# Gated DeltaNet in a hybrid decoder trunk: channel-major outputs by swapped operands, norm factors applied late through DRAM

## The chip, the cores and the metric

The kernel runs on one core of a Trainium2 chip. The metric is the device time of one execution in microseconds; lower is better. A core has five engines with instruction queues of their own, each working in order: TensorE (PE, matrix products; its weight loads are listed as PEld), VectorE (DVE), ScalarE (ACT), GpSimd (POOL) and SyncE (SP, which here only issues DMA transfers; ACT and POOL issue some too).

## The reference, cut to what matters

One layer: RMS norm of 528 tokens (16 learned meta tokens and 512) of width 2048, one input projection, three groups of heads (gated DeltaNet 6 × 128, GLA 5 heads, forgetting attention "FoX" 5 heads), each with a SiLU gate, and one output projection with the residual and a last norm. All is fp32. The change lies in DeltaNet, whose output is normed and gated per head:

```
def gated_head_norm(o, z, w):
    o = o * lax.rsqrt(jnp.mean(o * o, axis=-1, keepdims=True) + EPS) * w
    return o.reshape(z.shape) * jax.nn.silu(z)
...
        v_new = u_c - jnp.einsum('bhck,bhkv->bhcv', w_c, s)
        o = jnp.einsum('bhck,bhkv->bhcv', qd, s) + jnp.einsum('bhcs,bhsv->bhcv', qk_c, v_new)
        s = s * gl[..., None, None] + jnp.einsum('bhck,bhcv->bhkv', kd, v_new)
```

The norm is a factor for each token and head; w is a factor for each channel; silu(z) has one value per channel and token.

## The kernel before, in words

The input projection runs in blocks of 128 columns, `pp20`, `pp21` and so on, each in two halves of the contraction. A half's weights come as 512 KB (`raw`, issued by SP at L144), ACT rounds them to a high part (`whi`, L167), DVE makes the rest (`wlo = raw − whi`, L168), and PE does 48 products of 264 columns (or 24 of 512) with them at L242: high by high, high by the input's rest, low by high. `raw`, `whi` and `wlo` have two buffers each, so the next half's weights can be loaded and split while one is in use, and not before. PE takes projection products nearly all the time; the small products of the mixers are put between them. That order, and the one on every engine, is set when the program is built, by a scheduler's simulated times with a few tables of places (`PLACE`, `waits`, `sooner`); on the chip each engine follows its list and waits for semaphores. A dependency of the kind NoSync, in the code, only sets the order in a list and makes nothing wait.

DeltaNet runs in two groups of three heads, g = 0 and 1: `dn_keys`, `dn_values`, `dn_queries`, `dn_inverse`, `dn_mix`. While one group is mixed, the projections of the next are already under way. In `dn_keys` DVE makes the columns of decays (`cols`, L704 to L709) and with them the chunks' lower triangles `an` (L723). `dn_inverse` writes `an` to DRAM (`scr`, ACT's DMAs at L735) and reads it back as rows of small triangles (`ab`, L740); POOL fills ab's diagonal with ones (L744), and DVE inverts the triangles by steps (L749, L753). POOL's and DVE's other work stands around that: `stc5` on POOL, the convolution products `cv5` (L612, L614) and the next weight halves on DVE.

`dn_mix` goes over four blocks of 128 tokens: `pks` (keys by state), the correction `zz` on DVE, `py`, the state's update, and the output products `po`, of two products per head, token-major: tokens on partitions and channels along the row. ACT squares po with an accumulator (L975) and the norm's factors come from short DVE and ACT instructions; ACT scales po by them (L984). One block later, `gated` transposes each head on PE (`pt`, L902) and multiplies it by the channel weight and by the gate `zsdz`, which is channel-major, on DVE (L905). When a group is done, SP stores its three gates' rows to DRAM (`zd`, L1362), from where the output projection reads them.

The query's squared sums use a tile `qs` (one buffer, about the width of three heads) and a 128x128 matrix `fold`, which adds every fourth group of partitions; `fold` is made from the identity at L832 and L833 and lies in the tile `vpm`. Its product is `pq` (L891).

GLA works on pairs of heads. In `gla_pair` DVE makes the scaled keys and queries `kq` for spans of 64, 32, 16 and so on tokens (L1060 to L1067), and PE multiplies them to `pss` in four runs, `pss00` to `pss03` for the first pair (of two heads each, as `pss000` and `pss001`). POOL multiplies at L1111 and L1129 there.

Of the kernel before, what the change touches and what calls it, by code (L numbers as in the profile page):

```python
# [83 lines left out]
def tile_hybrid_trunk(ctx, tc, xT, x_first, w_first, xtok, mtok, w_gate, w_in, w_out, w_dn, consts, lmask, fin_w, out, dbg=None):  # L84
# [642 lines left out]

    def dn_inverse(g, st):
# [15 lines left out]
        G.memset(ab[:, 0:1024:33], 1.0)  # L744
        a3 = ab.rearrange("p (a c) -> p a c", a=32)
        for j in range(1, 31):
            m = 31 - j
            t3 = ot[:, : m * j].rearrange("p (a c) -> p a c", a=m)
            x = V.tensor_tensor(out=t3, in0=a3[:, j + 1 :, j : j + 1].to_broadcast([NN * 4 + H, m, j]),  # L749
                                in1=a3[:, j : j + 1, 0:j].to_broadcast([NN * 4 + H, m, j]), op=ALU.mult)  # L750
# [110 lines left out]
    def dn_mix(g, st):  # L861
# [37 lines left out]
        def gated(b):  # L899
            pt = psm.tile([P, 512], F32, tag="m", name=f"pt{g}{b}")  # L900
            for j in range(H):
                PE.transpose(pt[:, j * P : (j + 1) * P], ons[b][:, j, :], ident)  # L902
            for j in range(H):
                o = zs["dz", H * g + j][:, b * P : (b + 1) * P]
                V.scalar_tensor_tensor(out=o, in0=pt[:, j * P : (j + 1) * P], scalar=dnws[:, 0:1], in1=o,  # L905
                                       op0=ALU.mult, op1=ALU.mult)
# [9 lines left out]
        def scores(b):  # L916
            ts = bsl(b)
            p1 = psm.tile([P, 512], F32, tag="m", name=f"pa{g}{b}")
            for j in range(H):
# [2 lines left out]
            V.tensor_tensor(out=atb, in0=p1[:, : H * P].rearrange("p (h d) -> p h d", h=H), in1=atb, op=ALU.mult)
# [8 lines left out]
        scores(0)
        for b in range(NB):
            ts, eg, egl = bsl(b), egs[b], egls[b]
# [32 lines left out]
            if b:  # L966
                gated(b - 1)
            po = psm.tile([P, 512], F32, tag="m", name=f"po{g}{b}")
            for j in range(H):
# [1 line left out]
                PE.matmul(pj, at[:, b * H + j, :], y[:, j, :], start=True, stop=False)
# [8 lines left out]
            V.tensor_tensor(out=f1, in0=f1, in1=f2, op=ALU.add)  # L980
            A.activation(f1, f1, AF.Exp, scale=-0.5)
            on = t15(f"on{g}{b}")
            for j in range(H):
                A.activation(on[:, j, :], po[:, j * P : (j + 1) * P], AF.Copy, scale=f1[:, j : j + 1])  # L984
# [363 lines left out]
    for g in range(2):  # L1348
# [12 lines left out]
        for h in range(H * g, H * g + H):  # L1361
            nc.sync.dma_start(out=zd[h], in_=zs["dz", h])  # L1362
# [368 lines left out]
```

## Time and profile before

| what | us |
|---|---|
| three runs, median (lowest to highest) | 966.07 (965.44 to 967.99) |
| the profiled execution | 966.72 |
| its span, first to last instruction | 964.8 |
| PE busy | 955.4 |
| DVE busy | 688.2 |
| ACT busy | 474.5 |
| POOL busy | 233.0 |

The TensorE clock was granted in full (0.999). The span is what the trace covers; 1.9 us of the execution lie outside it. PE's busy time overlaps itself from one product to the next, since they are pipelined; what a product costs is the distance to the start of the next one.

### The profile page before, as it was taken

The numbers are of one execution on the slowest core, as the hardware profiler recorded it, in microseconds if no ns is written. First come the engines' busy times: TensorE is split into PE (matmuls) and PEld (weight loads), VectorE is DVE, ScalarE is ACT, GpSimd is POOL, SyncE is SP. The second block draws the span as 40 slices with busy tenths as digits, with TensorE's granted clock in tenths as the row PEclk, the third lists the DMA queues.
The fourth block names the chain that finished last, engine by engine and source line by source line (L and its number), as shares of the span: only waits on it lengthen the run. The fifth ranks groups of instructions, "written<-read, shape, count | busy, mean of one in ns | idle before, by whom it ended". The sixth has DMA issues, their size and how long they took to land.

```text
span 964.8 us, 18868 instructions
## 1 busy us (share of the span) xinstructions
PE 955.4 (99%) x7271; PEld 882.4 (91%) x7271; DVE 688.2 (71%) x1491; ACT 474.5 (49%) x1004; POOL 233.0 (24%) x262
## 2 busy tenths in 40 slices
PE   9999999999999999999999999999999999999996
PEld 8899999899999988899999989899999998888885
DVE  5467777878658886634685857968867758986664
ACT  7754433344446333433545554655655645544345
POOL 0033322233124235211112223232433120000023
PEclk9999999999999999999999999999999999999999
DMA  9835577978558787743747675678776588366535
GB/s 355 298 136 209 180 205 212 287 227 227 171 167 221 226 233 192 188 119 83 186 133 179 158 185 180 187 216 225 190 210 175 181 285 281 131 218 217 178 128 175
DMA packets 70334, 191.86 MB, mean 199 GB/s; under 512 B 14077, under 2 KB 17325, under 8 KB 69476
## 3 DMA queue, kind: packets, MB, share of 16 engines
q1 hardware_dynamic: 46048, 152.64, 45.5%
q0 software_dynamic: 15104, 31.66, 18.5%
q10 hardware_dynamic: 9092, 6.36, 2.5%
q8 instruction: 57, 0.93, 0.4%
q14 instruction: 33, 0.27, 0.1%
HBM read 179.94 MB, written 60.88 MB: 250 GB/s over the span
## 4 chain that ended last, share of the span: by engine, by line
PE 97%; DVE 1%; DMA 1%; ACT 0%; issue 0%; POOL 0%; ACTq 0%; SPq 0%; DVEq 0%; POOLq 0%
PE pp L242 48%; PE pp_a L569 8%; PE pq L1452 6%; PE pp L321 5%; PE pa L1452 3%; PE pt L1452 3%; PE ps L1452 3%; PE pp_b L569 2%; PE pp_c L569 2%; PE pp_d L569 2%; PE pr L1452 1%; PE pss L1087 1%; PE pfo L1328 1%; PE pfa L1279 1%; PE pgate L415 1%; PE pg L716 1%
## 5 line engine op out<-in xcount | busy, mean ns | idle before, releaser
L242 PE MATMUL pp<-xh,whi 128*128 128x264 f32 (+2 forms) x1120 | 269.6, 305 | 0.0
L242 PE MATMUL pp<-xl,whi 128*128 128x264 f32 (+2 forms) x1120 | 269.6, 305 | 0.0
L242 PE MATMUL pp<-xh,wlo 128*128 128x264 f32 (+2 forms) x1120 | 268.4, 305 | 0.2 <-DVE wlo L168 0.2
L167 ACT CAST whi<-raw 128x1024 fp32r<-128x1024 f32 x131 | 137.2, 1047 | 158.8 <-PE pp L242 97.3
L168 DVE TENSOR_TENSOR wlo<-raw,whi 128x1024 fp32r<-128x1024 f32 x131 | 165.0, 1260 | 62.6 <-ACT whi L167 59.9
L242 PEld LDWEIGHTS pp<-xh,whi 128*128 128x128 f32 x1120 | 181.2, 188 | 8.9 <-issue 0.3
L242 PEld LDWEIGHTS pp<-xl,whi 128*128 128x128 f32 x1120 | 181.5, 189 | 8.4
L242 PEld LDWEIGHTS pp<-xh,wlo 128*128 128x128 f32 x1120 | 181.1, 189 | 8.8 <-DVE wlo L168 0.5
L374 POOL TENSOR_SCALAR stc<-cv 128x528 f32<-128x528 f32 (+1 forms) x18 | 29.0, 1614 | 104.1 <-DVE cv L614 88.1
L614 DVE SCALAR_TENSOR_TENSOR cv<-pb,cpk,cv 128x528 f32<-128x528 f32 (+1 forms) x54 | 40.8, 756 | 0.6
L168 DVE TENSOR_TENSOR wlos<-raws,whis 128x1024 fp32r<-128x1024 f32 x20 | 24.2, 1222 | 14.6 <-ACT whis L167 14.6
L167 ACT CAST whis<-raws 128x1024 fp32r<-128x1024 f32 x20 | 20.7, 1049 | 26.8 <-PE pq L1452 12.5
L321 PE MATMUL pp<-xh,wf 128*128 128x512 f32 x128 | 33.1, 398 | 0.0
L1481 POOL TENSOR_TENSOR acc<-acc,fw 128x512 f32<-128x512 f32 x4 | 6.1, 1544 | 107.9 <-DVE wll L168 107.9
L569 PE MATMUL pp_a<-t,whi 128*128 128x264 f32 (+1 forms) x224 | 29.7, 282 | 0.0
L321 PEld LDWEIGHTS pp<-xh,wf 128*128 128x128 f32 x128 | 24.2, 190 | 5.6
L569 PE MATMUL pp_a<-xl,whi 128*128 128x264 f32 x112 | 28.5, 287 | 0.0
L569 PE MATMUL pp_a<-xh,whi 128*128 128x264 f32 x112 | 28.4, 286 | 0.0
L569 PEld LDWEIGHTS pp_a<-t,whi 128*128 128x128 f32 x224 | 27.8, 188 | 0.1
L363 DVE TENSOR_TENSOR pb<-pp,rstd 128x264 f32<-128x264 f32 (+1 forms) x36 | 13.8, 424 | 18.1 <-PE pp L242 18.0
L374 POOL TENSOR_SCALAR stdz<-zdz 128x512 f32<-128x512 f32 x6 | 11.2, 1874 | 62.5 <-DMA ti<-in_w_in 50.0
L481 POOL DMA_DIRECT2D tw<-tw x16 | 13.4, 835 | 51.7 <-DVE wlo L168 25.3
(497 smaller groups left out, 2072.8 us busy)
## 6 DMA issues: line engine op xcount, KB each, us to landing
raw<-in_w_in SPq DMA_DIRECT2D x103, 512.0 KB, 3.9
ti<-in_w_in SPq DMA_DIRECT2D x28, 512.0 KB, 5.2
raw<-ti SPq DMA_DIRECT2D x28, 512.0 KB, 3.5
tw<-in_w_dn SPq DMA_DIRECT2D x20, 512.0 KB, 5.3
raws<-tw SPq DMA_DIRECT2D x15, 512.0 KB, 4.0
ti<-in_w_in POOLq DMA_DIRECT2D x14, 512.0 KB, 6.3
ti<-ti POOLq DMA_DIRECT2D x14, 512.0 KB, 6.3
tw<-in_w_dn POOLq DMA_DIRECT2D x10, 512.0 KB, 6.6
```

The source lines that it names most:

```text
L167: pace[0] = A.copy(hi, raw).ins
L168: pace[1] = V.tensor_tensor(out=lo, in0=raw, in1=hi.bitcast(F32), op=ALU.subtract).ins
L242: mm = PE.matmul(p_[:, :nt], wt[:, j * m : (j + 1) * m], xx[k][:, t0 : t0 + nt], start=(k == 0 and wt is hi and xx is xh), stop=(k == KT - ...
L321: PE.matmul(begun[i][0][0][:, :S], wt[:, i * P : (i + 1) * P], xx[k][:, NM:T], start=k + n == 0, stop=k == KT - 1 and n == 2)
L363: V.tensor_tensor(out=o, in0=p_[rows], in1=rstd[rows, t0 : t0 + n], op=ALU.mult)
L374: maxes.append(G.tensor_scalar_max(t, src, LOW).ins)
L415: PE.matmul(pgate[a][:, :HT], wg[k // 8][:, k % 8, :], xx[k][:, a * HT : (a + 1) * HT], start=(k == 0 and xx is xh), stop=(k == KT - 1 and ...
L481: x = G.dma_start(out=out_[s], in_=in_[s], accum_op=ALU.add, max_dma_last_dim=2048)
L569: m = PE.matmul(p_[:, cols], wt[:, j * P : (j + 1) * P], xx[j][part_][:, cols], start=first and i == 0, stop=i == len(todo) - 1, skip_grou ...
L614: V.scalar_tensor_tensor(out=c, in0=pb[:, t0 + w : w + T], scalar=cwc[:, blk, w : w + 1], in1=c, op0=ALU.mult, op1=ALU.add)
L716: PE.matmul(pg[:r, j * r : (j + 1) * r], kT[:, j, ts], kT[:, j, ts], start=True, stop=True)
L1452: mm = PE.matmul(p_, o_[:, s], w_, start=(first and n == 0), stop=(last and n == 2), skip_group_check=True)
```

## The change

In `dn_mix` the two operands of the output products change places: `y` and the state are the stationary operands, and `at` and `eg` the moving ones, so po comes out channel-major. The gate is then multiplied into it at once, without the norm: `zb` gets po × channel weight × gate, in one DVE instruction per block. For the norm, DVE transposes po in blocks of 32x32 into `ot`, ACT squares it, and DVE sums 32 at a time (`squares`); the sums of all four blocks are folded by one product `pqo` per group (`normed`), which replaces the chain per block. The 12x128 factors are transposed (`pf`), copied (`ft`), stored to DRAM by four SP transfers (`fd`) and read back spread over all partitions (`fb`, 128x1536) into the buffer of tag "qs". POOL multiplies the gates by them in `gate` (three products of 128x512), and SP stores the result. For the first group that is done at once; for the second it is written behind the scores of GLA's first pair, with a NoSync dependency on the last `kq`.

Three smaller moves go with it: `fold` is made inside the tile `qs` instead of `vpm`; ab's diagonal is filled by DVE; the copy of the decays `egl` and POOL's product with `eg` come behind the corrections `zz`, and `squares` of a block behind those of the next.

```diff
+    factors = []
+
+    def gate(behind):
+
+        for g, zt, fb in factors:
+            for j in range(H):
+                x = G.tensor_tensor(out=zt[:, j, :S], in0=zt[:, j, :S], in1=fb[:, j], op=ALU.mult)
+                if behind:
+                    tc.add_manual_dep(x.ins, behind.name, mybir.DependencyInfo(
+                        mybir.DependencyClass.NoSync, mybir.DependencyReason.DATA), reason="behind")
+            for j in range(H):
+                nc.sync.dma_start(out=zd[H * g + j], in_=zt[:, j, :S])
+        factors.clear()
+
@@ -741,7 +755,7 @@
-        G.memset(ab[:, 0:1024:33], 1.0)
+        V.memset(ab[:, 0:1024:33], 1.0)
@@ -824,14 +838,10 @@
-        vpm3 = t15(f"vpm{g}")
+        vpm3 = t15(f"vpm{g}", (P, 2, P))
         vpm = vpm3[:, 0]
         vms = vpm3[:, 1]
         G.memset(vms, 0.0)
-        fold = vpm3[:, 2].rearrange("p (i a) -> p i a", i=4)
-        V.reduce_sum(fold[:, 0], ident.rearrange("p (i a) -> p a i", a=32), axis=mybir.AxisListType.X)
-        V.tensor_copy(fold[:, 1:], fold[:, 0].unsqueeze(1).to_broadcast([P, 3, 32]))
-        st["fold"] = vpm3[:, 2]
@@ -874,12 +884,28 @@
+        def squares(b):
+
+            return V.reduce_sum(st["sums"][:, 4 * H * b : 4 * H * (b + 1)],
+                                ots[b].rearrange("p h (i c) -> p (h i) c", c=32), axis=mybir.AxisListType.X)
+
+        zt = triples["dz", g]
-            sums = qs[:, H * S : H * S + 16 * H].rearrange("p (h m) -> p h m", h=H)
+            sums, st["sums"], st["fold"] = (qs[:, H * S + a : H * S + b] for a, b in ((0, 16 * H), (16 * H, 32 * H), (32 * H, 32 * H + P)))
+            f4 = st["fold"].rearrange("p (i a) -> p i a", i=4)
+            V.reduce_sum(f4[:, 0], ident.rearrange("p (i a) -> p a i", a=32), axis=mybir.AxisListType.X)
+            V.tensor_copy(f4[:, 1:], f4[:, 0].unsqueeze(1).to_broadcast([P, 3, 32]))
@@ -896,14 +922,31 @@
-        def gated(b):
-            pt = psm.tile([P, 512], F32, tag="m", name=f"pt{g}{b}")
-            for j in range(H):
-                PE.transpose(pt[:, j * P : (j + 1) * P], ons[b][:, j, :], ident)
-            for j in range(H):
-                o = zs["dz", H * g + j][:, b * P : (b + 1) * P]
-                V.scalar_tensor_tensor(out=o, in0=pt[:, j * P : (j + 1) * P], scalar=dnws[:, 0:1], in1=o,
-                                       op0=ALU.mult, op1=ALU.mult)
+        def normed():
+
+            pq = psm.tile([P, 512], F32, tag="m", name=f"pqo{g}")
+            PE.matmul(pq[:, : 16 * H], st["fold"], st["sums"], start=True, stop=True)
+            for i in range(4):
+                r = slice(32 * i, 32 * i + 32)
+                A.copy(so_[r], pq[r, : 16 * H].rearrange("p (b h i) -> p b h i", h=H, i=4)[:, :, :, i])
+            f1, f2 = f_[:, 0], f_[:, 1]
+            V.tensor_tensor(out=f2, in0=f2, in1=so_, op=ALU.mult)
+            A.activation(f2, f2, AF.Ln, scale=1.0 / (P * P), bias=eps_c)
+            V.tensor_tensor(out=f1, in0=f1, in1=f2, op=ALU.add)
+            A.activation(f1, f1, AF.Exp, scale=-0.5)
+            pf = psm.tile([P, 512], F32, tag="m", name=f"pf{g}")
+            PE.transpose(pf[: NB * H, :P], f1.rearrange("p b h -> p (b h)"), ident)
+            ft = t15(f"ft{g}", (NB * H, P))
+            A.copy(ft, pf[: NB * H, :P])
+            fd = drp.tile([H, NB, P], F32, name=f"fd{g}")
+            for b in range(NB):
+                nc.sync.dma_start(out=fd[:, b], in_=ft[b * H : b * H + H])
+            fb = wk.tile([P, 2 * T + 2 * S], F32, tag="qs", bufs=1, name=f"fb{g}")[:, : H * S]
+            fb = fb.rearrange("p (h t) -> p h t", h=H)
+            nc.sync.dma_start(out=fb, in_=fd.rearrange("h b t -> h (b t)").partition_broadcast(P))
+            factors.append((g, zt, fb))
+            if g == 0:
+                gate(None)
@@ -923,14 +966,11 @@
-            egl = wk.tile([P, H], F32, tag="egl", name=f"egl{g}{b}")
-            V.tensor_copy(egl, eg[:, :, P - 1])
-            G.tensor_tensor(out=eg, in0=eg, in1=qT[:, :, ts], op=ALU.mult)
-            egs[b], egls[b] = eg, egl
@@ -938,8 +978,13 @@
+                x = V.scalar_tensor_tensor(out=z[:, j, :], in0=pk[:, j * P : (j + 1) * P], scalar=nbg[:, b, j : j + 1],
+                                           in1=vp[:, b * H + j, :], op0=ALU.mult, op1=ALU.add)
+            egl = wk.tile([P, H], F32, tag="egl", name=f"egl{g}{b}")
+            behind(V.tensor_copy(egl, eg[:, :, P - 1]), x)
+            G.tensor_tensor(out=eg, in0=eg, in1=qT[:, :, ts], op=ALU.mult)
+            if b:
+                behind(squares(b - 1), x)
@@ -963,29 +1008,22 @@
-            if b:
-                gated(b - 1)
             po = psm.tile([P, 512], F32, tag="m", name=f"po{g}{b}")
             for j in range(H):
                 pj = po[:, j * P : (j + 1) * P]
-                PE.matmul(pj, at[:, b * H + j, :], y[:, j, :], start=True, stop=False)
-                PE.matmul(pj, eg[:, j, :], sst[:, j, :], start=False, stop=True)
-            for j in range(H):
-                sq = wk.tile([P, P], BF16, tag="sq", name=f"sqo{g}{b}{j}")
-                A.activation(sq, po[:, j * P : (j + 1) * P], AF.Square, accum_out=so_[:, b, j : j + 1])
-
-            f1, f2 = f_[:, 0, b, :], f_[:, 1, b, :]
-            V.tensor_tensor(out=f2, in0=f2, in1=so_[:, b, :], op=ALU.mult)
-            A.activation(f2, f2, AF.Ln, scale=1.0 / (P * P), bias=eps_c)
-            V.tensor_tensor(out=f1, in0=f1, in1=f2, op=ALU.add)
-            A.activation(f1, f1, AF.Exp, scale=-0.5)
-            on = t15(f"on{g}{b}")
-            for j in range(H):
-                A.activation(on[:, j, :], po[:, j * P : (j + 1) * P], AF.Copy, scale=f1[:, j : j + 1])
-            ons[b] = on
+                PE.matmul(pj, y[:, j, :], at[:, b * H + j, :], start=True, stop=False)
+                PE.matmul(pj, sst[:, j, :], eg[:, j, :], start=False, stop=True)
+            ot = t15(f"ot{g}{b}")
+            V.transpose(ot.rearrange("p h t -> p (h t)"), po[:, : H * P])
+            zb = zt[:, :, b * P : (b + 1) * P]
+            V.scalar_tensor_tensor(out=zb, in0=po[:, : H * P].rearrange("p (h t) -> p h t", h=H), scalar=dnws[:, 0:1],
+                                   in1=zb, op0=ALU.mult, op1=ALU.mult)
+            A.activation(ot, ot, AF.Square)
+            ots[b] = ot
             if b < NB - 1:
                 sst = sn
-        gated(NB - 1)
+        squares(NB - 1)
+        normed()
@@ -1100,6 +1138,8 @@
+        if p == 0:
+            gate(kqs[-1])
@@ -1358,8 +1398,6 @@
-        for h in range(H * g, H * g + H):
-            nc.sync.dma_start(out=zd[h], in_=zs["dz", h])
```

What the orders become, at three places. First PE, at the second block of the first group, where `pt00` are the transposes of block 0's output (columns: line, operation, out<-in, shape, times). Before:

```order
L242 MATMUL pp20_0_3504<-xl4_222,whi20_0_3509 128x264
L957 MATMUL psn01_2342<-y01_2340,kd0_1056 128x128 x3
L920 MATMUL pa02_2350<-qT0_1663,kT0_672 128x128 x3
L902 MATMUL pt00_2361<-ident_79,on00_2324 128x128 x3
L971 MATMUL po01_2368<-y01_2340,at0_1057 128x128
L972 MATMUL po01_2368<-sn00_2292,eg01_2301 128x128
L971 MATMUL po01_2368<-y01_2340,at0_1057 128x128
L972 MATMUL po01_2368<-sn00_2292,eg01_2301 128x128
L971 MATMUL po01_2368<-y01_2340,at0_1057 128x128
L972 MATMUL po01_2368<-sn00_2292,eg01_2301 128x128
L242 MATMUL pp20_1_3505<-xl4_222,whi20_0_3509 128x264
```

After:

```order
L242 MATMUL pp20_0_3462<-xl4_222,whi20_0_3467 128x264
L1002 MATMUL psn01_2333<-y01_2331,kd0_1056 128x128 x3
L963 MATMUL pa02_2341<-qT0_1661,kT0_672 128x128 x3
L1014 MATMUL po01_2349<-at0_1057,y01_2331 128x128
L1015 MATMUL po01_2349<-eg01_2301,sn00_2292 128x128
L1014 MATMUL po01_2349<-at0_1057,y01_2331 128x128
L1015 MATMUL po01_2349<-eg01_2301,sn00_2292 128x128
L1014 MATMUL po01_2349<-at0_1057,y01_2331 128x128
L1015 MATMUL po01_2349<-eg01_2301,sn00_2292 128x128
L242 MATMUL pp20_1_3463<-xl4_222,whi20_0_3467 128x264
```

The three transposes are gone, and the six output products have the same places with their operands exchanged.

Then DVE in the second group, around the columns of decays and the diagonal of `ab1`; `wlo25_0` is the low part of the first half of block 25. Before:

```order
L706 COPY cols1_3042<-cols1_3042 128x12
L706 COPY cols1_3042<-cols1_3042 16x3
L707 COPY cols1_3042<-cols1_3042 128x12
L707 COPY cols1_3042<-cols1_3042 16x3
L839 COPY cols1_3042<-cols1_3042 16x1 x2
...
L612 TENSOR_SCALAR cv5_4015<-pb5_3898,cpk_90 128x512
L614 SCALAR_TENSOR_TENSOR cv5_4015<-pb5_3898,cpk_90,cv5_4015 128x512 x3
L168 TENSOR_TENSOR wlo25_0_4561<-raw25_0_4557,whi25_0_4560 128x1024
L749 TENSOR_TENSOR ab1_4026<-ab1_4026 51x30
L753 TENSOR_TENSOR ab1_4026<-ab1_4026 51x30
```

After:

```order
L706 COPY cols1_3002<-cols1_3002 128x12
L706 COPY cols1_3002<-cols1_3002 16x3
L906 TENSOR_REDUCE qs1_4209<-ident_79 128x32
L707 COPY cols1_3002<-cols1_3002 128x12
L707 COPY cols1_3002<-cols1_3002 16x3
...
L612 TENSOR_SCALAR cv5_3973<-pb5_3856,cpk_90 128x512
L758 MEMSET ab1_3984 51x32
L614 SCALAR_TENSOR_TENSOR cv5_3973<-pb5_3856,cpk_90,cv5_3973 128x512 x3
L168 TENSOR_TENSOR wlo25_0_4475<-raw25_0_4471,whi25_0_4474 128x1024
L763 TENSOR_TENSOR ab1_3984<-ab1_3984 51x30
L767 TENSOR_TENSOR ab1_3984<-ab1_3984 51x30
```

The fold's reduction now stands inside the chain of `cols`, where it needs the buffer in which `fb0` lay; the fill stands ahead of three products of `cv5` and of `wlo25_0`, where before DVE's first touch of `ab1` came behind them.

Last POOL, from the masks `at1` of the second group on; `zsdz0` are the first group's gates. Before:

```order
L695 AFFINE_SELECT at1_3035<-at1_3035 128x384 x2
L486 DMA ti_669<-ti_669 256x512
L695 AFFINE_SELECT at1_3035<-at1_3035 128x384
L374 TENSOR_SCALAR stc4_3892<-cv4_3887 128x512
L830 MEMSET vpm1_3215 128x128
L849 COPY vpm1_3215<-v3_3223 128x16
L849 COPY vpm1_3215<-v4_3362 128x16
L849 COPY vpm1_3215<-v5_3501 128x16
L732 MEMSET ab1_4026 51x1024
L486 DMA ti_669<-ti_669 256x512
L744 MEMSET ab1_4026 51x32
L374 TENSOR_SCALAR stc5_4020<-cv5_4015 128x512
```

After:

```order
L695 AFFINE_SELECT at1_2995<-at1_2995 128x384 x2
L734 TENSOR_TENSOR zsdz0_527<-zsdz0_527,fb0_2454 128x512 x3
L695 AFFINE_SELECT at1_2995<-at1_2995 128x384
L374 TENSOR_SCALAR stc4_3850<-cv4_3845 128x512
L844 MEMSET vpm1_3175 128x128
L859 COPY vpm1_3175<-v3_3181 128x16
L859 COPY vpm1_3175<-v4_3320 128x16
L859 COPY vpm1_3175<-v5_3459 128x16
L746 MEMSET ab1_3984 51x1024
L486 DMA ti_669<-ti_669 256x512
L374 TENSOR_SCALAR stc5_3978<-cv5_3973 128x512
```

The three products with `fb0` come ahead of the last mask, of `stc4` and of all that follows; the fill has left the queue, so that `stc5` no longer stands behind it.

More of the change, by code (lines that the diff above doesn't have):

```diff
@@ L752, in dn_inverse @@
                 waits.append((x.ins, len(splits) + 2, splits))
-            V.tensor_tensor(out=a3[:, j + 1 :, 0:j], in0=a3[:, j + 1 :, 0:j], in1=t3, op=ALU.add)
+            x = V.tensor_tensor(out=a3[:, j + 1 :, 0:j], in0=a3[:, j + 1 :, 0:j], in1=t3, op=ALU.add)
         sc2 = drp.tile([NN * 4, 1024], F32, tag="sc2", name=f"sc2{g}", bufs=2)
@@ L876, in dn_mix, with behind @@
         f_ = wk.tile([P, 2, NB, H], F32, tag="ff", name=f"ff{g}")
-        egs, egls, ons = {}, {}, {}
+        egs, ots = {}, {}
+        def behind(x, y):
+            tc.add_manual_dep(x.ins, y.ins.name, mybir.DependencyInfo(
+                mybir.DependencyClass.NoSync, mybir.DependencyReason.DATA), reason="behind")
+        def squares(b):
+            return V.reduce_sum(st["sums"][:, 4 * H * b : 4 * H * (b + 1)],
+                                ots[b].rearrange("p h (i c) -> p (h i) c", c=32), axis=mybir.AxisListType.X)
+        zt = triples["dz", g]
         def query_sums():
             qs = wk.tile([P, 2 * T + 2 * S], F32, tag="qs", bufs=1, name=f"qs{g}")
-            sums = qs[:, H * S : H * S + 16 * H].rearrange("p (h m) -> p h m", h=H)
+            sums, st["sums"], st["fold"] = (qs[:, H * S + a : H * S + b] for a, b in ((0, 16 * H), (16 * H, 32 * H), (32 * H, 32 * H + P)))
+            f4 = st["fold"].rearrange("p (i a) -> p i a", i=4)
+            V.reduce_sum(f4[:, 0], ident.rearrange("p (i a) -> p a i", a=32), axis=mybir.AxisListType.X)
+            V.tensor_copy(f4[:, 1:], f4[:, 0].unsqueeze(1).to_broadcast([P, 3, 32]))
+            sums = sums.rearrange("p (h m) -> p h m", h=H)
             for j in range(H):
@@ L925, in scores @@
             A.activation(eg, eg, AF.Exp)
-            egl = wk.tile([P, H], F32, tag="egl", name=f"egl{g}{b}")
-            V.tensor_copy(egl, eg[:, :, P - 1])
-            G.tensor_tensor(out=eg, in0=eg, in1=qT[:, :, ts], op=ALU.mult)
-            egs[b], egls[b] = eg, egl
+            egs[b] = eg
         scores(0)
         for b in range(NB):
-            ts, eg, egl = bsl(b), egs[b], egls[b]
+            ts, eg = bsl(b), egs[b]
             pk = psm.tile([P, 512], F32, tag="m", name=f"pks{g}{b}")
@@ L940, in dn_mix @@
             for j in range(H):
-                V.scalar_tensor_tensor(out=z[:, j, :], in0=pk[:, j * P : (j + 1) * P], scalar=nbg[:, b, j : j + 1],
-                                       in1=vp[:, b * H + j, :], op0=ALU.mult, op1=ALU.add)
+                x = V.scalar_tensor_tensor(out=z[:, j, :], in0=pk[:, j * P : (j + 1) * P], scalar=nbg[:, b, j : j + 1],
[5 more added lines that the diff above has]
+                behind(squares(b - 1), x)
             py = psm.tile([P, 512], F32, tag="m", name=f"py{g}{b}")
```

## The prediction

> **What bounds the kernel now.** I read the page's head first, then the chain that ended last, then what TensorE (PE) waits for.
>
> ```profile
> span 964.8 us, 18868 instructions
> PE 955.4 (99%) x7271; PEld 882.4 (91%) x7271; DVE 688.2 (71%) x1491; ACT 474.5 (49%) x1004; POOL 233.0 (24%) x262
> ...
> PE 97%; DVE 1%; DMA 1%; ACT 0%; issue 0%; POOL 0%; ACTq 0%; SPq 0%; DVEq 0%; POOLq 0%
> ```
> ```profile
> PE warm L310 <- POOL ones L115: 1.2, 1, 1.2
> PE pp L242 <- DVE wlo L168: 0.2, 1, 0.2
> PE pp_b L569 <- ACT whi L167: 0.2, 1, 0.2
> ```
>
> PE is busy 955.4 of 964.8 us, 97% of the chain is PE, and after the start it waits 0.4 us in all. So the time is the sum of PE's steps. A saving on DVE, ACT or POOL is worth nothing; PE work taken away is worth its step; and any new wait of PE is paid in full, since PE has no idle time that could take it up.
>
> **The PE work.** Behind block 1's state update the rows read (a busy figure overlaps the next row, so the step is the difference of starts):
>
> ```profile
> 266.79 0.49 PE L902 MATMUL pt<-ident,on 128*128 128x128 f32 x3
> 267.12 0.39 PE L971 MATMUL po<-y,at 128*128 128x128 f32 x2
> ```
> ```profile
> L902 PE MATMUL pt<-ident,on x24: 270/273/273, 266.8 to 476.5; 128*128 128x128 f32 x24
> ```
> ```profile
> L891 PE MATMUL pq<-qs,vpm x4: 208/242/276, 247.4 to 425.7; 128*128 128x48 f32 x4
> ```
>
> Three transposes take 267.12 − 266.79 = 0.33 us, 0.11 each; 24 go: −2.66 us. Swapping the operands of the output products leaves their count and shapes (128x128 both ways). Added per group are one 128x48 product with the fold matrix (the L891 kind, two passes of at most 0.14 by its two rows per group and 276 ns) and one transpose (0.11): +0.72 in all, a little under the most that these rows allow. PE's sum falls by 1.94 us; half of it, 0.97, lies in each group. At no cover at all that is the most the change can give, but for the 0.4 us of waits above.
>
> **Work beside PE, per block.** It removes three gatings, three squares with their accumulator reads and three scaled copies; it adds a 32x32-block transpose of 128x384, one gating of 128x384, one 128x384 square and one reduction.
>
> ```profile
> L905 DVE SCALAR_TENSOR_TENSOR zsdz<-pt,dnws,zsdz x24: 329/343/351, 267.6 to 477.3; 128x128 f32<-128x128 f32 x24
> L984 ACT ACTIVATE on<-po,ff x24: 346/367/373, 259.4 to 473.6; 128x128 f32<-128x128 f32 x24
> ```
> ```profile
> L767 DVE STREAM_TRANSPOSE iv<-iv x2: 578/580/581, 213.7 to 383.6; 128x384 f32<-128x384 f32 x2
> ```
> ```profile
> L922 DVE TENSOR_TENSOR at<-pa,at x8: 549/550/557, 241.6 to 454.6; 128x384 f32<-128x384 f32 x8
> L889 DVE TENSOR_REDUCE qs<-qs x6: 670/672/675, 218.3 to 392.1; 128x16 f32<-128x512 f32 x6
> ```
>
> ```profile
> 296.97 1.22 DVE L168 TENSOR_TENSOR wlo<-raw,whi 128x1024 fp32r<-128x1024 f32 x1
> ```
> ```profile
> 303.25 0.40 PE L242 MATMUL pp<-xh,wlo 128*128 128x258 f32 x2
> ```
>
> DVE: 0.58 + 0.55 + about 0.55 (between nothing and the 0.67 of a 128x512) against 3 × 0.34, so +0.6 us a block; ACT loses about 1.1 (three copies of 0.37). I cost them at nothing: the cover is the weights' lead (here the low part of a half is done at 298.2 and first used at 303.25, 5 us), and the corrections, on which PE waits next, keep their place ahead of the new work. Without that cover eight blocks would cost 8 × 0.6 = 4.8 us.
>
> **Where the second group's inverse now waits.** Two moves meet here: the fold matrix now lies in the buffer "qs", which the first group's factors fb0 hold until POOL has gated with them, and the fill of ab's diagonal goes from POOL to DVE, ahead of cv5's three products and wlo25_0. First, when is POOL done? The factors' transpose pf0 stands where the last block's pt stood, 13 projection steps of 0.12 us later, less the transposes saved: about 300.5.
>
> ```profile
> 300.08 0.27 PE L902 MATMUL pt<-ident,on 128*128 128x128 f32 x1
> ```
> ```profile
> 302.73 1.05 ACT L167 CAST whi<-raw 128x1024 fp32r<-128x1024 f32 x1
> ```
> ```profile
> 301.36 1.30 SPq L1362 DMA_DIRECT2D zd<-zsdz  x3
> 307.41 0.33 SPq L144 DMA_DIRECT2D raw<-in_w_in  x1
> ```
> ```profile
> L739 ACTq DMA_DIRECT2D scmeta<-anm x2: 308/308/309, 119.5 to 316.6; - x2
> ...
> DMA to landing us min/median/max: 2.0/2.0/2.0
> ```
> ```profile
> L655 ACTq DMA_DIRECT2D gb<-gd x2: 344/346/349, 72.7 to 214.3; - x2
> ...
> DMA to landing us min/median/max: 6.2/6.2/6.2
> ```
> ```profile
> L888 POOL TENSOR_TENSOR qs<-qs x6: 1032/1189/1587, 216.0 to 388.7; 128x512 f32<-128x512 f32 x6
> ```
>
> ACT copies ft0 behind whi23_0, which moves up a little from its 302.73: done at 303.2. SP issues four rows (0.43 each, 1.7) and the last lands 2.0 behind its issue: 306.7 to 306.9. The next weight half, which SP issued at 307.41, stands ahead of fb0; its low part comes earlier in the new DVE order, so I take fb0 at 306.8. It is a broadcast of 786 KB; the nearest, gb, took 6.2 us: 313.0. Three products of 128x512 at 1.03 to 1.59: 316.1 to 317.8.
>
> [...]
>
> ```profile
> 314.77 0.23 DVE L706 COPY cols<-cols 128x12 f32<-128x12 f32 x2
> 314.96 0.67 DVE L707 COPY cols<-cols 128x12 f32<-128x12 f32 x2
> ...
> 327.78 0.47 DVE L612 TENSOR_SCALAR cv<-pb,cpk 128x512 f32<-128x512 f32 x1
> 328.29 2.33 DVE L614 SCALAR_TENSOR_TENSOR cv<-pb,cpk,cv 128x512 f32<-128x512 f32 x3
> 331.85 1.23 DVE L168 TENSOR_TENSOR wlo<-raw,whi 128x1024 fp32r<-128x1024 f32 x1 [1.23 <-ACT whi L167]
> 333.50 0.20 DVE L749 TENSOR_TENSOR ab<-ab 51x30 f32<-51x30 f32 x1 [0.43 <-DMA ab<-scr]
> ```
> ```profile
> 333.52 0.15 POOL L744 MEMSET ab<- 51x32 f32 x1 [14.38 <-DMA ab<-scr]
> ```
> ```profile
> 336.81 0.40 PE L242 MATMUL pp<-xh,wlo 128*128 128x512 f32 x1
> ```
>
> The new fold reduction stands between L706 and L707, at 314.96. It can start at 316.1 to 317.8 and its neighbour products on DVE slow POOL meanwhile; I take 317.3, 2.3 us late (1.0 to 2.9; with POOL products of 2.46, a row quoted below, up to 5.3). All that follows is in one chain: cols, an, the write to scr, and its reading back into ab, which landed at about 333.43 (just before DVE's start at 333.50): 335.7. Until now only POOL waited there (14.38 us, at no cost). Now DVE waits with the fill, and behind it stand cv5's products (2.33) and wlo25_0 (1.23): 335.73 + 0.15 + 2.33 + 1.23 = 339.4. PE needs wlo25_0 at 336.81 − 0.97 = 335.84. So PE waits 3.6 us. With the fill alone and no lateness ahead of it: 333.43 + 3.71 − 335.84 = 1.3; with 5.3 late, 6.6. The next halves follow at PE's pace, and I add nothing for them.
>
> **GLA's first keys.** POOL gates the second group in the middle of DVE's making of the first keys kq, and the products pss010 and pss020 now follow each other with no projection steps between.
>
> ```profile
> 489.74 0.16 DVE L1119 TENSOR_TENSOR gdm<-gqk 128x16 f32<-128x16 f32 x1
> ...
> 491.83 1.28 DVE L1121 TENSOR_TENSOR gdm<-gdm,gqk 128x16 f32<-128x16 f32 x1
> ```
> ```profile
> 490.62 2.46 POOL L1111 TENSOR_TENSOR gt<-gt,gqk 128x512 f32<-128x512 f32 x1 [12.28 <-ACT gt L1110]
> ```
> ```profile
> L1129 POOL TENSOR_TENSOR gqk<-gqk x3: 1290/1304/1308, 509.4 to 618.6; 128x512 f32<-128x512 f32 x2, 64x512 f32<-64x512 f32 x1
> ```
> ```profile
> 501.18 0.42 DVE L1067 TENSOR_TENSOR kq<-gqk,gpr 128x256 f32<-128x256 f32 x1
> ```
> ```profile
> 502.21 1.16 PE L1087 MATMUL pss<-kq 64*64 64x64 f32 x64
> ```
>
> Beside DVE's dense chain a POOL product took 2.46 instead of 1.30, and one 128x16 subtraction on DVE took 1.28 instead of 0.16: 1.1 us lost once per POOL product. Three products cost DVE up to 3.3 us. In hand are 502.21 − 501.60 = 0.6, and pss020's place is 12 projection steps, 1.5 us, later than before (pss000 29 later, the runs behind it 26 and 0 in place of 19 and 24): 2.1. So PE waits between 0 and 3.3; I take 3.3 − 2.1, rounded down to 1.0.
>
> [...]
>
> **Sum.** −1.94 + 3.6 + 1.0 = +2.7 us. The profiled run took 966.72 (964.8 of it the span), 0.65 over the median 966.07 and inside the runs' 965.44 to 967.99; from the median: 968.7.
>
> **Rivals.** About 0.3%, 2.9 us, is what a measurement of this kernel can tell from no change. A, on the other side: the projection halves behind the inverse are fed from a longer lead than I read, so that a late wlo25_0 costs PE nothing, and only the saving is left: 964.1, less up to 0.4 of the waits above. It decides from a lead of 3.6 us more at 336; for it, other halves do have 5 us; against it, this one has 333.08 to 336.81, 3.7, all of which the chain uses up. Chance 0.13. B: the fold reduction finds its buffer free, as POOL's gating ends before 315, and the fill alone waits: −1.94 + 1.3 + 0.5, 965.9. Chance 0.16. [...] C, the fold 5.3 us late, as POOL's products meet DVE's and take 2.46 each: −1.94 + 6.6 + 1.0 = +5.7, 971.7. It decides from fb0 landing after 314. Chance 0.10. D, three whole POOL products lost in front of the keys: −1.94 + 3.6 + 3.3 = +5.0, 971.0. It decides if kq has nothing in hand there. Chance 0.10.
>
> **Numbers.** My own case has 0.51, from 966.9 to 970.5. The range 964.2 to 972.2 leaves out half of A and the far ends of C and D. Slower by over 2.9 us (above 968.97) is half of my case and nearly all of C and D: 0.45. Faster (below 963.17) needs more than PE's saving: 0.06. The rest, 0.49.
>
> **What would show it.** No L902 row and 18 PE instructions fewer; a wait of PE on wlo at L168 of 2 to 6 us near 336; DVE's fold reduction (L906) idle ahead of it on POOL, near 315; DVE's fill (L758) idle on ab<-scr; POOL's products (L734) at 1.3 to 2.5 us, and a wait of PE on kq in the first pair. I would be wrong if L906 or L758 stood without idle time, if the waits hit halves with lead enough, or if PE waited elsewhere, most likely at the weights behind 26.

## The result and the profile after

The changed kernel takes 980.17 us (median of 5 runs, 977.52 to 981.83) against 966.38 us (5 runs, 965.44 to 967.99): a ratio of 1.0135 (of the means of these runs), 95% interval 1.0121 to 1.0149. By the medians it is 13.8 us slower; 2.7 us were forecast, and the range ended at 972.2. The profiled execution after took 980.17 us, 978.5 of it the span.

The head of the page after, and the first lines of its chain of work:

```profile
span 978.5 us, 18781 instructions
PE 958.0 (98%) x7253; PEld 883.5 (90%) x7253; DVE 699.1 (71%) x1481; ACT 464.8 (48%) x938; POOL 241.8 (25%) x266
...
PE 85%; DVE 5%; DMA 4%; issue 3%; ACT 1%; POOL 1%; ACTq 0%; SPq 0%; POOLq 0%; DVEq 0%
```

PE's share of the chain that ended last has fallen from 97% to 85%: PE now waits for others.

What PE waits for, after (total, times, longest, us):

```profile
PE pp L242 <- DVE wlo L168: 4.0, 1, 4.0
PE pss L1125 <- DVE kq L1105: 3.4, 2, 1.8
PE pg L716 <- DVE anm L723: 2.4, 1, 2.4
PE warm L310 <- POOL ones L115: 1.2, 1, 1.2
PE pp_a L569 <- ACT vf L584: 1.1, 1, 1.1
PE pp_b L569 <- ACT whi L167: 0.3, 1, 0.3
```

Before, these waits made 1.6 us; now 12.4, so +10.8. PE has 18 instructions fewer, yet is busy 2.6 us longer (958.0 against 955.4). Together 13.4 of the 13.7 us of span. Work worth 1.9 us went away, so some products must be slower by 4.5 us in all. Four places hold nearly all of it: pg at 321, wlo at 342, kq at 511 and 514, vf at 638. These lines, like all that follow, are of one profiled execution of each kernel, which can lie up to 2.0 us from the median of its runs.

**The second group's inverse.** DVE and POOL, first before, then after:

```profile
312.48 0.74 DVE L614 SCALAR_TENSOR_TENSOR cv<-pb,cpk,cv 128x512 f32<-128x512 f32 x1
313.14 0.23 DVE L704 TENSOR_TENSOR cols<-cols 128x12 f32<-128x12 f32 x2
...
316.02 0.50 DVE L723 SCALAR_TENSOR_TENSOR anm<-pg,cols,e 16x16 f32<-16x16 f32 x3
```
```profile
307.34 0.68 DVE L717 TENSOR_SCALAR e<-gb,gcol 128x128 f32<-128x128 f32 x3 [1.99 <-DMA fd<-ft]
...
313.72 1.82 DVE L614 SCALAR_TENSOR_TENSOR cv<-pb,cpk,cv 128x512 f32<-128x512 f32 x1
315.47 1.31 DVE L704 TENSOR_TENSOR cols<-cols 128x12 f32<-128x12 f32 x2
316.71 1.79 DVE L614 SCALAR_TENSOR_TENSOR cv<-pb,cpk,cv 128x512 f32<-128x512 f32 x1
...
319.71 0.35 DVE L906 TENSOR_REDUCE qs<-ident 128x32 f32<-128x128 f32 x1
...
321.04 0.50 DVE L723 SCALAR_TENSOR_TENSOR anm<-pg,cols,e 16x16 f32<-16x16 f32 x3
```
```profile
313.71 4.24 POOL L734 TENSOR_TENSOR zsdz<-zsdz,fb 128x512 f32<-128x512 f32 x3 [1.76 <-DMA fb<-fd]
```

The fold reduction (L906) has no idle time ahead of it: when DVE reaches it at 319.71, POOL has been done for 1.8 us. What is late is DVE itself. While POOL's three products run, two L614 take 1.82 and 1.79 instead of 0.74 and two small L704 1.31 instead of 0.23: 3.2 us. Before that DVE waits 2.0 us at L717, since e213 takes the pool slot of ft0, which is free only when the rows fd0 have left; 1.2 of it are left at the first L614 (313.72 against 312.48). An L705 of 0.55 instead of 0.23 and L906 itself, which now stands in the row, make up the rest of the 5.0 us by which anm is late. PE is the first to feel it, then DVE with its fill:

```profile
321.60 0.94 PE L716 MATMUL pg<-kT 128*128 128x128 f32 x6 [2.35 <-DVE anm L723]
```
```profile
339.04 0.74 DVE L614 SCALAR_TENSOR_TENSOR cv<-pb,cpk,cv 128x512 f32<-128x512 f32 x1 [6.34 <-DMA ab<-scr]
339.06 0.09 DVE L758 MEMSET ab<- 51x32 f32 x1
...
341.28 1.22 DVE L168 TENSOR_TENSOR wlo<-raw,whi 128x1024 fp32r<-128x1024 f32 x1
```
```profile
342.55 0.79 PE L242 MATMUL pp<-xh,wlo 128*128 128x512 f32 x1 [4.03 <-DVE wlo L168]
...
347.39 0.40 PE L242 MATMUL pp<-xl,whi 128*128 128x512 f32 x1
```

pg waits for one of the four PSUM buffers, which anm's instructions free. At the fill the memset (L758) and the first product start within 0.02 us of each other, after DVE has waited 6.34 us for ab. Behind the wait for wlo, 11 steps take 347.39 − 342.55 = 4.84 us, where 11 × 0.232 = 2.55 is usual (0.232: the distance of such rows from 347.39 on): 2.3 us more. Busy times by stretch after (PE, PEld, DVE, ACT, POOL, then the granted clock, the DMA share and GB/s) show why:

```profile
320.00:325.00 5.00, 3.40 (x30) 3.41 (x31) 4.96 (x22) 1.90 (x3) 3.75 (x7) 1.00 0.14 37
340.00:345.00 5.00, 2.45 (x6) 1.97 (x7) 4.69 (x12) 1.09 (x2) 3.20 (x2) 0.55 0.31 112
515.00:520.00 5.00, 5.00 (x120) 4.52 (x115) 3.90 (x11) 1.14 (x2) 0.00 (x0) 0.70 0.19 67
```

The clock is at 0.55 behind the wait of 4.03 us and at 1.00 behind that of 2.35.

**GLA's first keys**, DVE, POOL and PE after:

```profile
506.14 4.42 DVE L168 TENSOR_TENSOR wlo<-raw,whi 128x1024 fp32r<-128x1024 f32 x1
```
```profile
505.39 4.08 POOL L734 TENSOR_TENSOR zsdz<-zsdz,fb 128x512 f32<-128x512 f32 x3
```
```profile
511.28 1.37 PE L1125 MATMUL pss<-kq 64*64 64x64 f32 x64 [1.78 <-DVE kq L1105]
514.23 2.17 PE L1125 MATMUL pss<-kq 64*64 64x64 f32 x64 [1.58 <-DVE kq L1105]
516.33 0.59 PE L242 MATMUL pp<-xl,whi 128*128 128x264 f32 x1
```

One low part on DVE, 1.22 us elsewhere, takes 4.42: it begins at 506.14 beside the POOL products and ends at 510.56, 1.1 us behind the third of them (509.47). The keys come 3.2 us late, PE waits twice, and its 64 products take 1.37 and 2.17 instead of the 1.16 of before, with the clock at 0.70: another 1.2 (not all of it need be the clock: in e14, below, the first takes 1.37 too, at a clock of 1.00). Four rows of steps behind them, 516.33 to 518.04, take 1.7 instead of some 0.9: 0.8 more.

### The profile page after: what moved, and what is told of

The parts are those of the page before. It is cut to its first block, busy times and chain, and to the rows that moved or that the text cites. A ratio compares the mean times of both kernels' runs of the same rounds, so it can differ in the third digit from the quotient of the medians.

```text
span 978.5 us, 18781 instructions
## 1 busy us (share of the span) xinstructions
PE 958.0 (98%) x7253; PEld 883.5 (90%) x7253; DVE 699.1 (71%) x1481; ACT 464.8 (48%) x938; POOL 241.8 (25%) x266
## 4 chain that ended last, share of the span: by engine, by line
PE 85%; DVE 5%; DMA 4%; issue 3%; ACT 1%; POOL 1%; ACTq 0%; SPq 0%; POOLq 0%; DVEq 0%
PE pp L242 39%; PE pp_a L569 7%; PE pq L1490 6%; PE pp L321 5%; PE pa L1490 3%; PE pt L1490 3%; PE ps L1490 3%; PE pp_d L569 2%; PE pp_b L569 2%; PE pp_c L569 2%; PE pr L1490 1%; DVE wlo L168 1%; DMA zd<-gqk 1%; DMA fqk<-gd 1%; PE pss L1125 1%
## 5 line engine op out<-in xcount | busy, mean ns | idle before, releaser
L168 DVE TENSOR_TENSOR wlo<-raw,whi 128x1024 fp32r<-128x1024 f32 x131 | 167.3, 1277 | 52.3 <-ACT whi L167 47.6
L614 DVE SCALAR_TENSOR_TENSOR cv<-pb,cpk,cv 128x528 f32<-128x528 f32 (+1 forms) x54 | 43.0, 796 | 7.1 <-DMA ab<-scr 6.3
L168 DVE TENSOR_TENSOR wlos<-raws,whis 128x1024 fp32r<-128x1024 f32 x20 | 24.2, 1220 | 14.9 <-ACT whis L167 14.9
L167 ACT CAST whis<-raws 128x1024 fp32r<-128x1024 f32 x20 | 20.6, 1050 | 27.7 <-PE pq L1490 10.7
L985 POOL TENSOR_TENSOR eg<-eg,qT 128x384 f32<-128x384 f32 x8 | 8.1, 1017 | 83.0 <-DVE egl L984 79.6
L375 ACT ACTIVATE stc<-stc 128x528 f32<-128x528 f32 (+1 forms) x18 | 11.5, 639 | 33.9 <-POOL stc L374 19.9
```

The costliest lines, as they stand in the source:

```text
L167: pace[0] = A.copy(hi, raw).ins
L168: pace[1] = V.tensor_tensor(out=lo, in0=raw, in1=hi.bitcast(F32), op=ALU.subtract).ins
L375: A.activation(t, t, AF.Exp, scale=-1.0)
L614: V.scalar_tensor_tensor(out=c, in0=pb[:, t0 + w : w + T], scalar=cwc[:, blk, w : w + 1], in1=c, op0=ALU.mult, op1=ALU.add)
```

## The experiments

Every time below is a median with its range; the ratio is that of the means, with its 95% interval, to the kernel before, whose median in these comparisons lay at 965.99 to 966.70.

**e1, the fill back on POOL**

```diff
-        V.memset(ab[:, 0:1024:33], 1.0)
+        G.memset(ab[:, 0:1024:33], 1.0)
```

> The changed kernel with ab's diagonal filled by POOL again. In the changed kernel PE waited 4.0 us for wlo25_0 and then worked some 4 us at a low clock (2.3 us more). If DVE's wait in the fill is the cause, both go, as wlo25_0 would end near 336.5 and is needed at 338.4: about 974. Rival: the inverse is 5 us late anyway, its steps then hold up later weight halves, and PE waits there instead: 978 to 980.

975.79 us (973.6 to 976.4), ratio 1.0093 (1.0077 to 1.0109). The wait for wlo falls from 4.0 to 0.5 us. The gain is 4.4 us, 1.8 less than I expected; 3.5 of it are the wait, and the low clock does not go but moves: here the wait at pg, though shorter, is followed by it.

```profile
320.49 0.94 PE L716 MATMUL pg<-kT 128*128 128x128 f32 x6 [2.11 <-DVE anm L723]
```
```profile
320.00:325.00 5.00, 4.51 (x26) 4.51 (x27) 5.00 (x19) 1.89 (x3) 2.64 (x7) 0.67 0.22 32
```

**e2, the fold in buffers of its own.** It is made in a third plane of vpm, and again beside ft for the second sum; make_fold is the reduction and the copy that made it before.

```diff
-        vpm3 = t15(f"vpm{g}", (P, 2, P))
+        vpm3 = t15(f"vpm{g}")
+        st["fold"] = make_fold(vpm3[:, 2])
...
-            PE.matmul(pq[:, : 16 * H], st["fold"], st["sums"], start=True, stop=True)
+            ft = t15(f"ft{g}", (P, 2, P))
+            PE.matmul(pq[:, : 16 * H], make_fold(ft[:, 1]), st["sums"], start=True, stop=True)
...
```

> The changed kernel with the fold matrix for the queries in the tile vpm as before, and a second one made beside ft for the outputs. The prediction's theory, that the fold's reduction waits for POOL's gating, says 2 to 3 us of the second group's inverse come back, and PE's wait at wlo25_0 shrinks from 4.0 to 1 to 2 us: about 977. The rival, from the trace after: the reduction did not wait, the lateness is DVE's own work made slow beside POOL's products, so nothing changes: 980, within 1 us.

977.42 us (975.7 to 978.98), ratio 1.0119 (1.0102 to 1.0137). The number fits the step on record, but not by its reason, and the wait for wlo25_0 fell to 2.65 us and not to the 1 to 2 expected. Slots and order moved with the tile, DVE does not wait at L717 any more, and its products stand ahead of POOL's. So e2 tells little of the fold; e14 and e15 below take its place.

**e4, the second group's gate behind the pair's last masked copy**

```diff
-                        V.copy_predicated(a64[:, en], masked((16, 8, 4, 2, 1, 0).index(s), NB), pc)
+                        last = V.copy_predicated(a64[:, en], masked((16, 8, 4, 2, 1, 0).index(s), NB), pc)
         if p == 0:
-            gate(kqs[-1])
+            gate(last.ins)
```

> The changed kernel with the second group's gating by POOL put behind the last masked copy of GLA's first pair instead of behind the last keys. If POOL's three products, by blocking one DVE subtraction (wlo37_1, 4.4 us in place of 1.2), made the keys late, both waits for kq (3.4 us) and the low clock behind them go: 975 to 976. Rival: the new order of pss010 and pss020 alone makes them wait: 979 to 980.

975.84 us (975.35 to 976.98), ratio 1.0099 (1.0084 to 1.0114): 4.3 us back. The wait for kq falls from 3.4 to 0.6, and the clock from 515 to 520 is 1.00. Not all of the gain is this edit's place, though. In this execution the clock behind pg's wait (2.48 us) was 0.76 and then 0.90 in the two stretches from 320 to 330, PE came 1.4 us later to wlo25_0, and waited 2.1 us there instead of 4.0.

**e11, POOL busy at the same place, but without reading** (the second group's factors are left out of the output)

```diff
-                x = G.tensor_tensor(out=zt[:, j, :S], in0=zt[:, j, :S], in1=fb[:, j], op=ALU.mult)
+                xs_ = [G.memset(fb[:, j], 1.0) for _ in range(3)] if behind else []
...
```

> The changed kernel, but POOL fills fb1 nine times (128x512, writes only) where it multiplied the second group's gates three times, for about the same 4 us at the same place; the second group's norm factors are left out of the output. If DVE is blocked by what POOL reads, wlo37_1 takes 1.2 us again in place of 4.4 and the waits for kq shrink below 1 us: 975 to 976. If POOL's place in time or its being busy is enough, wlo37_1 stays above 3 us: 979 to 980.

974.19 us (972.75 to 974.83), ratio 1.0082 (1.0066 to 1.0099). DVE and POOL:

```profile
505.38 1.21 DVE L168 TENSOR_TENSOR wlo<-raw,whi 128x1024 fp32r<-128x1024 f32 x1
```
```profile
504.60 4.57 POOL L734 MEMSET fb<- 128x512 f32 x9
```

POOL is busy for 4.57 us beside the same low part, which now takes 1.21 instead of 4.42; the wait for kq is 0.7, and the clock behind it 1.00. So neither the place nor the load explains the time; what differs is that POOL reads: the low part takes 4.42 us beside products, which read two tiles each, and 1.21 beside fills, which only write. What in the chip holds the low part up, no run shows.

**e14, the same for the first group** (the first group's factors are left out of the output)

```diff
-                x = G.tensor_tensor(out=zt[:, j, :S], in0=zt[:, j, :S], in1=fb[:, j], op=ALU.mult)
+                if behind:
+                    x = G.tensor_tensor(out=zt[:, j, :S], in0=zt[:, j, :S], in1=fb[:, j], op=ALU.mult)
+                else:
+                    for _ in range(3):
+                        G.memset(fb[:, j], 1.0)
```

> POOL writes ones into the first group's factor buffer nine times, once the factors have landed there, instead of its three products, so the first group's norm factors are left out of the output. POOL is busy as long and at the same place, but reads nothing. Theory: 3.3 of the 5.0 us by which anm is late come from DVE instructions blocked by the reads of POOL's products, and 2.0 from DVE's wait for the slot of ft. Then DVE's corrections near 314 take 0.73 and L704 0.23, the wait of 2.0 at L717 stays, anm comes 3 us earlier (318 instead of 321.0), PE does not wait at pg (2.4 before), the wait for wlo stays near 3 us with the low clock behind it: 977 (976 to 978). Rival, that POOL's products have no part in the lateness: anm at 321 and 980.

976.80 us (976.13 to 978.38), ratio 1.0105 (1.0090 to 1.0120). DVE:

```profile
307.76 0.68 DVE L717 TENSOR_SCALAR e<-gb,gcol 128x128 f32<-128x128 f32 x3 [1.86 <-DMA fd<-ft]
...
314.15 0.74 DVE L614 SCALAR_TENSOR_TENSOR cv<-pb,cpk,cv 128x512 f32<-128x512 f32 x1
...
317.66 0.50 DVE L723 SCALAR_TENSOR_TENSOR anm<-pg,cols,e 16x16 f32<-16x16 f32 x3
```

POOL writes from 314.28 to 319.04, and DVE's rows have their usual length (two L704 0.22): anm comes at 317.66 instead of 321.04. PE no longer waits at pg. So 3.4 of the 5.0 us go with POOL's reads, some 0.2 of them because the fold's reduction has moved out of the row; the wait of 1.86 at L717 stays, and 1.6 us of lateness with it. The wait for wlo stayed at 4.0, not the 3 I expected: ACT's four issues of scr<-an took 4.82 us there against 2.18 after, and gave back part of what anm had gained. At GLA's keys, where this kernel is as the changed one, PE again waits 1.78 and then 1.58 us, but here the clock stays at 1.00 from 510 to 520.

**e15, ft in free columns of qs**

```diff
...
-            ft = t15(f"ft{g}", (NB * H, P))
+            ft = st["ft"][: NB * H]
```

> The transposed factors ft go into unused columns of qs instead of a buffer of the pool that e also takes its buffers from. The order moves with it: the rows e stand ahead of the factors, and the factors' products some 20 projection steps later on PE. Theory: DVE no longer waits 2.0 us at L717; POOL's products come later too and still block DVE, but fall on other rows. If they fall behind cols and anm, PE does not wait at pg, and the wait for wlo is that of the fill, 1.3 to 2: 975 to 976. If they still fall ahead of anm, about 978. Rival (the record's step): the fold, now the reduction behind an, waits for POOL and delays what stands behind it, 977 to 980, with a visible wait of DVE on POOL at L906.

976.73 us (974.88 to 977.24), ratio 1.0103 (1.0086 to 1.0120). The wait at L717 is gone, as is that at pg; anm comes at 316.11, though POOL still stretched two tiny instructions just ahead of it (1.10 and 1.05 us, 0.23 together before):

```profile
313.85 1.10 DVE L709 TENSOR_TENSOR cols<-cols 128x12 f32<-128x12 f32 x1
...
316.11 0.50 DVE L723 SCALAR_TENSOR_TENSOR anm<-pg,cols,e 16x16 f32<-16x16 f32 x3
...
318.61 0.37 DVE L906 TENSOR_REDUCE qs<-ident 128x32 f32<-128x128 f32 x1
```

L906 again has no idle time: in this order too, the wait that the step on record expected there does not show. Waits for wlo of 3.3 in three places (longest 2.1) and for kq of 3.5 remain, 0.7 us more in the sum than I expected.

**e7 and e8, a pause alone.** The kernel before, with an idle DVE reduction of 18 (e8: 23) × 528 columns, 10.04 and 12.80 us, between wlo24_1 and wlo25_0; one run each.

> The kernel before, with one idle reduction of 18 rows of 528 on DVE (about 9.9 us, its result unused) between wlo24_1 and wlo25_0, so that PE has to wait about 2.6 us for wlo25_0. If a pause of PE by itself lowers its granted clock, steps behind the wait take more than the 0.23 us of before for some microseconds; with a pause this short I expect none or little, as behind the changed kernel's 2.4 us wait at pg: clock 1.00 in the ten microseconds behind it, time about 966.4 + 2.6 = 969.

> The same with 23 rows (12.7 us), so that PE waits about 5.4 us. If the pause lowers the clock, steps of 0.43 us in place of 0.23 follow for about 4 us and the loss is 2 us more than the wait: about 974. If the low clock of the changed kernel came from something else there, only the wait is lost: about 972.

971.29 us (e7) and 973.30 us (e8). PE of e7, then of e8:

```profile
338.35 0.50 PE L249 MATMUL pp<-xh,wlo 128*128 128x512 f32 x1 [2.47 <-DVE wlo L175]
...
339.61 0.63 PE L249 MATMUL pp<-xh,whi 128*128 128x512 f32 x1
340.04 0.63 PE L249 MATMUL pp<-xl,whi 128*128 128x512 f32 x1
...
342.80 0.40 PE L249 MATMUL pp<-xh,wlo 128*128 128x512 f32 x1
```
```profile
341.43 0.80 PE L249 MATMUL pp<-xh,wlo 128*128 128x512 f32 x1 [5.21 <-DVE wlo L175]
...
346.70 0.39 PE L249 MATMUL pp<-xh,wlo 128*128 128x512 f32 x1
```

I expected no drop behind 2.47 us, and was wrong: the steps go from 0.232 to 0.43 us some 0.8 us after the restart, until 342.56 (the row at 342.80 is at the usual step again); the granted clock from 340 to 345 is 0.75 in e7 and 0.50 in e8. Between the two rows of e8 lie 12 steps: 5.27 us instead of 12 × 0.232 = 2.8. In e7 the 11 steps from 338.35 to 342.56 take 4.2 instead of 2.6. So a pause of 2.5 us cost 4.1 there, and one of 5.2 cost 7.7. (e8 is 7.3 over the 965.99 of before; e7 5.3, as a wait for vf of 0.9 came with it.)

**e6, e10, e12: the causes mended together.** e6 has the fill on POOL, the fold of e2, the second group's gate as in e4, and the first group's behind the last product that makes an for group 1:

```diff
+        if g == 1:
+            gate(last.ins)
...
-            if g == 0:
-                gate(None)
```

e10 takes e6 with the fill on DVE again, but behind wlo25_0, and ft in a row buffer:

```diff
+        x = V.memset(ab[:, 0:1024:33], 1.0)
+        if g == 1:
+            waits.append((x.ins, len(splits) + 2, splits))
...
+            ft = row(f"ft{g}")
```

e12 takes e10 with one PSUM buffer fewer:

```diff
-            pf = psm.tile([P, 512], F32, tag="m", name=f"pf{g}")
+            pf = pq[:, P:]
```

> All repairs in one: fill on POOL, fold in vpm, the first group's gating behind the last product of the second group's triangles, the second group's behind GLA's last masked copy. If the stalls are the whole loss, the PE saving of 1.9 us is left, less a wait of 1.1 us on vf later: 964.5 to 966. If the swapped operands, the new DVE work or the factors' transfers cost PE time by themselves: 968 to 972.

> The kernel with all repairs, and two more: the diagonal is filled by DVE but behind wlo25_0, so that neither POOL's stc5 nor a weight half stands behind it, and ft lies in a row tile, so that e213 no longer waits for the transfers of fd0. If the 1.6 us that PE still waited for weights of blocks 25 and 26 came from these two, they go: 966 to 967, the same as before within 0.3%; with the waits for kq and vf still there (1.2 us) it does not beat it by more than 0.5.

> The kernel with all repairs, and the factors' transpose pf in the free columns of the bank of pqo, so that normed takes one bank of the four in place of two. With it the decay projection pgk and the keys of GLA's first pair stand as early again as before the change. If the bank was what put GLA's keys late, the waits for kq (1.1 us) go and PE's saving is kept up to GLA: 964.5 to 965.5, faster than before by about 1 us. Rival: the scheduler's later places are due to DVE's added work, the waits stay, 966 to 968.

e6: 968.67 us (967.01 to 974.84), ratio 1.0031 (1.0014 to 1.0048). e10: 968.88 us (965.98 to 972.11), 1.0027 (1.0014 to 1.0039). e12: 967.02 us (964.65 to 969.85), 1.0005 (0.9994 to 1.0016), no difference from before. All three lie above what I expected, by 2.7, 1.9 and 1.5 us from its upper end; e6 and e12 lie in the ranges of their rivals. For e6 the rival was that the new work costs PE time by itself; PE's busy time there, 953.9 us, is 1.5 less than before, and its waits, 4.0, are 2.4 more, so in that execution it is the waits. Most of the 13.8 us is back, but none of them kept the saving, and none is faster than the kernel before. PE's busy time in e12:

```profile
PE 954.5 (99%) x7253; PEld 879.5 (91%) x7253; DVE 699.0 (72%) x1485; ACT 464.0 (48%) x938; POOL 238.8 (25%) x266
```

PE is busy 0.9 us less than before and waits 3.8 instead of 1.6: beside the 1.2 at the start, 0.9 for wlo in two places, 0.9 for vf, 0.4 for kq and twice 0.2. Smaller waits elsewhere stand in for the mended ones. Which of them the rest of the time is due to, no run isolates.

**e13, the PSUM buffer alone in the changed kernel** (the diff of e12, and nothing else)

> The changed kernel with nothing but this: pf in the bank of pqo. POOL's three products stay in the middle of the keys, but the chain of the keys starts earlier against PE. If lateness of the keys is bank and port together, the waits for kq shrink from 3.4 to 1 or 2 us, with less low clock behind: 976 to 978. If only the port counts, 980.

"Port" there stands for what e11 measured, 4.42 us of the low part beside POOL's products and 1.21 beside its fills; that a port is behind it, no run shows.

979.06 us (975.01 to 981.49), ratio 1.0127 (1.0106 to 1.0148): no difference from the changed kernel. The waits moved, though: that for kq fell from 3.4 to 2.0, as I had expected, while those for wlo rose from 4.0 to 5.0 in four places. So the buffer alone wins no time; why e12 is 1.9 us below e10 stays open. One of the waits for wlo, of 3.27 us, was not followed by a low clock:

```profile
343.58 0.50 PE L242 MATMUL pp<-xh,wlo 128*128 128x512 f32 x1 [3.27 <-DVE wlo L168]
```
```profile
340.00:345.00 5.00, 1.73 (x8) 1.20 (x7) 3.96 (x9) 0.09 (x1) 2.42 (x2) 1.00 0.11 23
345.00:350.00 5.00, 4.62 (x21) 3.44 (x20) 3.91 (x10) 2.75 (x4) 2.32 (x2) 1.00 0.98 254
```

## Why the prediction was wrong, by its steps

- **PE's saving of 1.94: right.** Matching PE's products one by one in the two traces gives 0.97 in the first group's mix and 0.97 in the second. In e10, where no wait is followed by a low clock (1.00 from 5 to 970), PE is busy 953.5 us: 1.9 less than before.
- **The work beside PE at nothing: right.** No wait of PE lies in the blocks.
- **The factors' way: right, to 0.7 us.** pf0 stands at 300.4 (300.5 forecast), fb was issued at 307.29 (306.8), POOL began at 313.71 (313.0) and ended at 317.95 (316.1 to 317.8). From fb0's issue by SP to POOL's start 6.4 us passed, close to the 6.2 of gb on which the forecast stood. Rival B would have needed POOL done before 315, some 3 us sooner.
- **"The new fold reduction ... can start at 316.1 to 317.8": the step that failed first.** It treated POOL's products as something that DVE waits for at one row. DVE's rows around it took 3.2 us more beside them (in e14, where POOL only writes, anm comes 3.4 us earlier), and DVE had already waited 2.0 us at L717 for the slot of ft0 (gone in e15), a slot of a pool that the prediction does not name. anm was 5.0 late, not 2.3. The record did say that POOL's neighbours meet it, but charged that to POOL (rival C: 2.46 a product); POOL took 1.41 a product and DVE paid.
- **PE between anm and the fill, not in the sum: 2.4 us** at pg, for the PSUM buffer that anm frees. I had followed anm's chain to ab and not to PE.
- **The fill: mechanism right.** 3.6 forecast, 4.0 measured, with the row of L758 as announced. Part of that is chance: wlo25_0 was done 3.1 us later than forecast (342.5), and PE needed it 2.7 later (338.5), as it had already lost 2.4 at pg.
- **GLA's keys: mis-sized, 1.0 against 3.4.** The loss per product was right (3 × 1.1; measured 3.2 in one row). The credit of 2.1 was wrong: the second product of the pair waits again by itself, 1.58. That is rival D, which had 0.10, and its 3.3. 2.7 of the 3.4 go away with POOL's reads (e11).
- **A wait of PE can cost more than its length: not in the sum, where it is the largest gap.** 2.3 us behind wlo and 2.0 around the keys: 4.3 of the 4.5 us by which products are slower (the rest of the difference in busy time). Not every wait does: 3.27 us in e13 and the two waits at the keys in e14 had a clock of 1.00 behind them.
- **vf: 1.1 us, open.** ACT makes vf at 624 before and at 638 after, behind transfers of xe. It was 0.05 us early before, and late by 0.2 to 1.8 in most of the variants, but also by 0.9 in e7, which has none of the change: so a shift in time alone can bring it. No run isolates it.

The record's sum was −1.94 + 3.6 + 1.0. Measured in the span: −1.9 + 2.4 (pg) + 4.0 (wlo) + 3.4 (kq) + 1.1 (vf) + 4.5 (slower products) − 0.1 (the small waits) = 13.4 of 13.7. The sum on record thus fell 10.7 short: 4.5 by the slower products, 2.4 at pg, 2.4 by the size of kq's wait, 1.1 by vf, 0.4 by wlo's, less 0.1.

## What to carry to other kernels

Where PE is 97% of the chain, ask of every moved instruction not just who waits for its result, but whose rows take longer while it runs: three POOL products that read beside a dense DVE stretch cost DVE 3.2 us at both places of the changed kernel, and 1.9 in the order of e15. Follow a late result to everything that it frees, PSUM buffers and pool slots too, and price each new PE wait of 2 us or more at its length and between nothing (e13) and 2.5 us (e8) besides. A saving of 0.2%, 1.9 us here, is less than one such wait.
